# Experts of a mixture-of-experts trunk: gate and up in one product of 512 columns, halves of rows in 4 KB pieces, splits of 1024 columns, the last matrix wholly split

## The chip, the cores and the metric

The kernel runs on 1 core of one Trainium2 chip. The metric is the device time of one execution in microseconds (us). The time of the kernel before is the median of 3 runs; beside them stands one profiled execution, from which every row below comes.

## The reference

Two layers of a post-norm encoder: 512 tokens of 1024 channels. Each layer has a token mixer (an input projection, two attention branches, an output projection) and then the mixture of experts, which the change is about. For each token a router picks one group of four experts and the two best experts in it; every expert is a gated unit of 256 channels.

```python
def _moe(h, w_router, router_bias, w_gate, w_up, w_down):
    t = h.reshape(b * s, d)
    scores = jax.nn.sigmoid((t @ w_router).astype(jnp.float32))
    sel = scores + router_bias.astype(jnp.float32)
    ...
    combine = jnp.sum(jax.nn.one_hot(idx, N_EXPERTS, dtype=jnp.float32) * gate[..., None], 1)
    hg = jnp.einsum('td,edf->tef', t, w_gate)
    hu = jnp.einsum('td,edf->tef', t, w_up)
    act = jax.nn.silu(hg) * hu * combine[..., None].astype(t.dtype)
    y = jnp.einsum('tef,efd->td', act, w_down)
    return y.reshape(b, s, d)
```

Per layer there are 16 experts, each with w_gate and w_up of 1024 x 256 and w_down of 256 x 1024 numbers, all fp32: three matrices of 1 MB, 48 MB per layer.

## The kernel before

**Products in halves.** An fp32 product is made from three cheaper ones. A matrix W is split into H, its copy rounded to the type fp32r, and L = W - H, also kept as fp32r; the activations are split in the same way, and the product is the sum xH·wH + xH·wL + xL·wH (`gemm3`, L220 to L227). For a weight the rounding copy runs on ACT (`ACT.copy`, L215) and the subtraction on DVE (`V.tensor_sub`, L216), both in `wsplit`, in pieces of 512 columns (two blocks of 256). The pieces rotate through `NWH` = 6 buffers with the tag `wH` and 6 with `wL`.

**Experts.** The loop over the 16 experts stands at the end of `layer`. For expert e it runs `x_gate(e)`, `x_down(e - 1)`, `x_up(e)` and `x_split(e + 1)`.

- `x_load` gathers the up to 128 rows of the tokens of an expert from DRAM (`h2d`) into `xe`, with an indirect DMA that POOL issues (L1104).
- `x_split` turns `xe` with eight transposes on TensorE (`tp`) and splits the result from PSUM into `xH` on ACT (L343) and `xL` on DVE (L344), each in two halves of four blocks.
- `x_prod` (called by `x_gate` and `x_up`) loads and splits one matrix and multiplies: for each of 8 blocks of 128 channels three matmuls of 256 columns, 24 for gate and 24 for up. Gate's result goes through Silu on ACT (`ea`, L1129) and is multiplied by up's on DVE (L1136).
- `x_down` turns `ea`, makes `eT`, `eH` and `eL` of it, and multiplies with w_down in two stretches of 512 columns. The constant `DS` names the parts of w_down that are split; the first stretch is not split and is multiplied in plain fp32 (L1173, `mm<-raw,eT`), the second stretch takes six split matmuls. DVE scales the result (`ye`, L1174) and POOL stores it with an indirect DMA (L1178).

**What sets the order.** The code names the work; a scheduler orders each engine's instructions when the program is built, and every engine then runs its own list strictly in that order, with semaphores between engines. `tc.issue_after` is a hint to that scheduler. A branch (`overflow`, taken only when an expert has more than 128 tokens) stands ahead of expert `EIF` = 5 and closes the first of two scheduled stretches.

**Loads.** w_gate and w_up are read as eight blocks of 128 rows, so that each DMA piece is one row of 256 numbers (1 KB); rows of w_down are pieces of 4 KB. The raw matrices rotate through 4 buffers `raw` and 5 buffers `e8`. `AHEADW` lists twelve matrices that are loaded ahead of the loop.

**Ahead of the experts.** For each of four token tiles `tile_x1` normalizes the mixer's result and `tile_h2` normalizes it again with the layer's modulation (`norm`, columns up to `CUTH` = 896 on DVE, the other 128 on ACT and POOL) and writes it to `h2d`. `stats` reckons mean and deviation with DVE, and POOL makes the reciprocal root (L285, L286). The last tile's root feeds the router's scores `rt_sco`; from these DVE and TensorE reckon the list of rows `vt`, and with `vt` POOL gathers the first expert's tokens. TensorE waits for that.

## Time and profile before

| | |
|---|---|
| median of 3 runs | 1416.98 us (1414.26 to 1420.2) |
| the profiled execution's own time | 1411.59 us |
| its span in the trace | 1409.6 us |
| its mean granted TensorE clock | 0.954 of 2.4 GHz |

The profile shows one execution. A page gives the busy time of the engines; views by stage give the same for a stretch of the span, with the granted clock of TensorE and the load of the 16 DMA engines; a list in order of time shows single instructions, with the idle time ahead of them in square brackets and what ended it. TensorE is written PE, VectorE DVE, ScalarE ACT, GpSimd POOL. Matmuls overlap in the trace: from one's start to the next one's start is what one costs.

### The profile page before, as it was taken

How to read it: one execution, taken by the hardware profiler on the slowest of the kernel's cores; microseconds unless marked ns; L12 is line 12 of the kernel's file. 1: busy time of each engine (PE TensorE's matmuls, PEld its weight loads, DVE VectorE, ACT ScalarE, POOL GpSimd, SP SyncE). 2: the span in 40 equal slices, each digit the busy share in tenths (PEclk: the TensorE clock that was granted, in tenths of full speed). 3: DMA queues.
4: the chain of work that ended last, by engine and by line, in shares of the span. 5: the costliest groups of instructions: out<-in, count | busy, mean ns of one | idle time of the engine just before them, and what ended most of it. 6: DMA issues, size and time to landing. Idle time of an engine off the chain costs nothing. (4 is left out here: it accounts for less than half of the span.)

```text
span 1409.6 us, 21666 instructions
## 1 busy us (share of the span) xinstructions
PE 1283.9 (91%) x7953; PEld 1043.7 (74%) x7953; DVE 1018.3 (72%) x1944; ACT 717.1 (51%) x1504; POOL 292.8 (21%) x317
## 2 busy tenths in 40 slices
PE   4898999999998949899889899999999894989986
PEld 4787777677778848788659787767777794878862
DVE  5877877776367779899787876563336767879985
ACT  2344444555744337677554444455564532767760
POOL 1142000000013652222352200000000266122224
PEclk9799999999999969999999999999999996999998
DMA  9646555466066197899644454122215527779952
GB/s 319 213 151 248 197 179 172 150 190 192 30 195 209 60 299 255 275 346 333 240 144 150 150 179 150 61 75 76 75 51 173 196 75 255 263 255 347 355 207 79
DMA packets 182992, 266.77 MB, mean 189 GB/s; under 512 B 18665, under 2 KB 131721, under 8 KB 182880
## 3 DMA queue, kind: packets, MB, share of 16 engines
q1 hardware_dynamic: 159312, 225.46, 48.2%
q0 software_dynamic: 11456, 24.07, 4.9%
q10 hardware_dynamic: 12112, 15.78, 3.7%
q8 instruction: 66, 1.08, 0.3%
q14 instruction: 46, 0.38, 0.1%
HBM read 250.79 MB, written 27.30 MB: 197 GB/s over the span
## 5 line engine op out<-in xcount | busy, mean ns | idle before, releaser
L216 DVE TENSOR_TENSOR wL<-raw,wH 128x512 fp32r<-128x512 f32 x520 | 350.8, 703 | 75.6 <-ACT wH L215 64.3
L215 ACT CAST wH<-raw 128x512 fp32r<-128x512 f32 x520 | 318.3, 622 | 160.2 <-PE mm L1173 41.6
L225 PE MATMUL mm<-hH,wH 128*128 128x512 f32 x512 | 206.9, 404 | 0.0
L226 PE MATMUL mm<-hL,wH 128*128 128x512 f32 x512 | 202.9, 396 | 0.0
L227 PE MATMUL mm<-hH,wL 128*128 128x512 f32 x512 | 202.5, 395 | 0.0
L225 PE MATMUL mm<-wH,xH 128*128 128x256 f32 x512 | 150.5, 294 | 2.0 <-ACT xH L343 1.2
L227 PE MATMUL mm<-wH,xL 128*128 128x256 f32 x512 | 149.4, 292 | 0.7 <-DVE xL L344 0.7
L226 PE MATMUL mm<-wL,xH 128*128 128x256 f32 x512 | 147.4, 288 | 0.7 <-DVE wL L216 0.7
L249 DVE SCALAR_TENSOR_TENSOR acc<-araw,cond,acc 128x512 f32<-128x512 f32 x148 | 110.8, 749 | 5.4 <-DMA araw<-in_w_ada 2.2
L227 PEld LDWEIGHTS mm<-hH,wL 128*128 128x128 f32 x512 | 96.4, 188 | 21.0 <-issue 1.1
L225 PEld LDWEIGHTS mm<-hH,wH 128*128 128x128 f32 x512 | 96.7, 189 | 20.2 <-issue 1.2
L226 PEld LDWEIGHTS mm<-hL,wH 128*128 128x128 f32 x512 | 96.6, 189 | 19.2 <-issue 0.3
L225 PEld LDWEIGHTS mm<-wH,xH 128*128 128x128 f32 x512 | 100.5, 196 | 4.3 <-ACT xH L343 2.1
L226 PEld LDWEIGHTS mm<-wL,xH 128*128 128x128 f32 x512 | 100.0, 195 | 2.6 <-DVE wL L216 1.4
L227 PEld LDWEIGHTS mm<-wH,xL 128*128 128x128 f32 x512 | 99.7, 195 | 1.6 <-DVE xL L344 1.1
L225 PE MATMUL mm<-wH,hH 128*128 128x256 f32 (+1 forms) x272 | 81.5, 300 | 4.8 <-ACT hH L412 3.1
L227 PE MATMUL mm<-wH,hL 128*128 128x256 f32 (+1 forms) x272 | 80.8, 299 | 2.0 <-DVE hL L378 0.7
L226 PE MATMUL mm<-wL,hH 128*128 128x256 f32 (+1 forms) x272 | 80.3, 296 | 0.1
L1178 POOL DMA_INDIRECT y<-ye,vt x28 | 33.5, 1198 | 221.8 <-DVE ye L1174 221.8
L281 POOL DMA_DIRECT2D mod<-adar x8 | 4.2, 531 | 331.1 <-ACT adar L280 331.1
L1173 PE MATMUL mm<-raw,eT 128*128 128x512 f32 x128 | 65.9, 639 | 5.1 <-ACT eT L1156 3.1
L745 DVE TENSOR_TENSOR zB<-sB,biasB 128x256 f32<-128x256 f32 (+2 forms) x48 | 22.9, 488 | 59.9 <-PE sB L743 26.1
(319 smaller groups left out, 2873.9 us busy)
## 6 DMA issues: line engine op xcount, KB each, us to landing
araw<-in_w_ada SPq DMA_DIRECT2D x44, 1024.0 KB, 5.3
raw<-in_w_in SPq DMA_DIRECT2D x40, 1024.0 KB, 5.2
raw<-in_w_exp_gate SPq DMA_DIRECT2D x32, 1024.0 KB, 8.7
raw<-in_w_exp_up SPq DMA_DIRECT2D x28, 1024.0 KB, 9.7
raw<-in_w_exp_down SPq DMA_DIRECT2D x28, 1024.0 KB, 7.5
raw<-in_w_out SPq DMA_DIRECT2D x8, 1024.0 KB, 5.2
y<-y SPq DMA_DIRECT2D x16, 512.0 KB, 8.0
eraw<-in_w_ada SPq DMA_DIRECT2D x4, 1024.0 KB, 14.6
```

The costliest lines, as they stand in the source:

```text
L215: ACT.copy(H, raw(s))
L216: V.tensor_sub(L, raw(s), H.bitcast(F32))
L225: PE.matmul(o, lhsT=lH, rhs=rH, start=(i == 0), stop=False)
L226: PE.matmul(o, lhsT=lH, rhs=rL, start=False, stop=False)
L227: PE.matmul(o, lhsT=lL, rhs=rH, start=False, stop=(i == n - 1))
L249: last = V.scalar_tensor_tensor(acc, raw[:, k, :], ck, acc, op0=OP.mult, op1=OP.add)
L281: PO.dma_start(moddr[l, kind].rearrange("o (k n) -> (o k) n", n=P), r[0:8, :])
L745: V.tensor_add(z, s[:, :, 0:wid], biasB[g][:, ii::2, j0:j0 + wid])
L1173: PE.matmul(p, lhsT=a, rhs=w, start=(i == 0), stop=(i == len(todo) - 1))
L1178: st = PO.indirect_dma_start(out=y2, out_offset=bass.IndirectOffsetOnAxis(ap=vidx[:, e:e + 1], axis=0), in_=ye, in_offset=None, bounds_che ...
```

## The change

Gate and up of an expert become one product. `x_raw` loads half of the rows of both (512 of 1024) side by side into one buffer of 128 x 2 x 4 x 256: a partition holds four neighbouring rows, so that each DMA piece is 4 KB, and each half is two DMAs of 512 KB. `x_prod(e, h)` splits such a half in two pieces of 1024 columns, and multiplies with 512 columns at a time (256 of gate, 256 of up) into one PSUM tile `gu`; two calls make 24 matmuls. Since the rows of the contraction are now numbered 4p + k, the activations' columns are written in that order by `norm_mixed`, which takes the place of `norm` in `tile_h2` and writes with a step of 128 columns.

`x_wdown` splits all of w_down into one pair of buffers `dH`, `dL` (one of each for all experts, taken from the `e8` pool): the copy on ACT, the subtraction on POOL. `x_down` has 12 split matmuls and no plain ones. The loop is `x_prod(e, 0)`, `x_down(e - 1)`, `x_wdown(e)`, `x_prod(e, 1)`, `x_act(e)`, `x_split(e + 1)`. All other weights are split in pieces of 1024 columns too, in 3 buffers each. Ten pieces of 1 MB are loaded ahead in place of twelve.

```diff
@@ wsplit
-            h = 512 // shape[1] if shape[1] < 512 else 1
+            h = min(a, 1024 // shape[1])
@@ 
+        def norm_mixed(src, name, g, b, st, q):
+            m, r, nb = st
+            n = f4(name, [D])
+            o = n.rearrange("p (h k q) -> p h q k", h=2, k=4)
+            view = lambda z: z.rearrange("p (h q k) -> p h q k", h=2, k=4)
+            x, g, b = view(src), view(g), view(b)
+            v = slice(q, P)
+            ACT.activation(o[:, 1, v], x[:, 1, v], AF.Identity, bias=nb, scale=r)
+            for h, u in ((0, slice(0, P)), (1, slice(0, q))):
+                V.scalar_tensor_tensor(o[:, h, u], x[:, h, u], m, g[:, h, u], op0=OP.subtract, op1=OP.mult)
...
+            PO.tensor_tensor(o[:, 1, v], o[:, 1, v], g[:, 1, v], op=OP.mult)
...
-                n2 = norm(n, "h2", r_sc2, r_sh2, st, CUTH)
+                n2 = norm_mixed(n, "h2", r_sc2, r_sh2, st, QH)
@@ layer
+                src = [z[512 * w:512 * w + 512].rearrange("(p k) n -> p k n", k=4) for z in (gate, up)]
...
+                raw = wp.tile([P, 2, 4, 256], F32, tag="raw", name="raw", bufs=NRAW) if tag == "raw" else e8("raw8", [2, 4, 256])
+                for i in range(2):
+                    SY.dma_start(raw[:, i], src[i])
+                return lambda j: raw[:, :, 2 * j:2 * j + 2]
...
+            def x_prod(e, h):
...
+                for j in range(2):
+                    H = wp.tile([P, 2, 2, 256], F32R, tag="wH", name="wH", bufs=NWH)
+                    L = wp.tile([P, 2, 2, 256], F32R, tag="wL", name="wL", bufs=NWH)
+                    with ExitStack() as order:
+                        if e == 0:
+                            order.enter_context(tc.issue_after(order1.ins))
+                        ACT.copy(H, raw(j))
+                        V.tensor_sub(L, raw(j), H.bitcast(F32))
+                    for i in range(2):
+                        k = 4 * h + 2 * j + i
+                        for n, (x, w) in enumerate(((xH, H), (xH, L), (xL, H))):
+                            PE.matmul(p, lhsT=x[:, k, :], rhs=w[:, :, i], start=(k == 0 and n == 0), stop=(k == 7 and n == 2))
+            def x_act(e):
...
+                ACT.activation(a, p[:, 0], AF.Silu)
+                V.tensor_mul(a, a, p[:, 1])
...
+            def x_wdown(e):
+                raw = x_src(e, "down")
+                for k in range(2):
+                    w = raw(slice(k, k + 1))[:, 0]
+                    with ExitStack() as order:
+                        if e == 0:
+                            order.enter_context(tc.issue_after(order1.ins))
+                        ACT.copy(dH[:, k], w)
+                        PO.tensor_tensor(dL[:, k], w, dH[:, k].bitcast(F32), op=OP.subtract)
...
+                    for k in range(2):
+                        for n, (x, w) in enumerate(((eH, dH), (eH, dL), (eL, dH))):
+                            PE.matmul(p, lhsT=x[:, k], rhs=w[:, k, js], start=(k == 0 and n == 0), stop=(k == 1 and n == 2))
...
-                x_gate(e)
+                x_prod(e, 0)
                 if e > 0:
                     x_down(e - 1)
-                x_up(e)
+                x_wdown(e)
+                x_prod(e, 1)
+                x_act(e)
@@ constants
-HOLD = 10
+HOLD = 9
-DS = ((0, 1), (1, 1))
-WPAT = ("e8",) * 5 + ("raw",) * 4
+WPAT = ("e8",) * 3 + ("raw",) * 4
-CUTH = 896
+QH = 96
-NWH = 6
+NWH = 3
```

**Order on ACT and DVE, one expert in the middle of the second stretch of layer 0.** Before, ACT's list from one Silu to the last split of the next tokens (`wH` with the same `raw` number belong to one matrix; `xH_6895` is the split of the next expert's tokens):

```order
L1129 ACTIVATE ea_6814<-mm_6789 128x256
L1156 COPY eT_6819<-tp_6816 128x256
L343 CAST eH_6821<-tp_6816 128x256
L215 CAST wH_6855<-raw8_6841 128x512
L343 CAST xH_6895<-tp_6897 128x512
L215 CAST wH_6887<-raw8_6885 128x512
L215 CAST wH_6891<-raw8_6885 128x512
L215 CAST wH_6916<-raw8_6914 128x512
L215 CAST wH_6920<-raw8_6914 128x512
L215 CAST wH_6924<-raw8_6914 128x512
L215 CAST wH_6928<-raw8_6914 128x512
L343 CAST xH_6895<-tp_6904 128x512
```

Now, from the split of this expert's tokens (`xH_6144`) to that of the next one's (`xH_6246`). `gu_6163` is this expert's product, `wH_6223` and `wH_6233` its second half, `wH_6269` and `wH_6279` the next expert's first half, `eH_6190` belongs to the expert before it, `raw8_6214` is this expert's w_down:

```order
L360 CAST xH_6144<-tp_6146 128x512
L360 CAST xH_6144<-tp_6153 128x512
L1167 CAST wH_6223<-raw8_6220 128x1024
L1167 CAST wH_6233<-raw8_6220 128x1024
L1167 CAST wH_6269<-raw8_6266 128x1024
L360 CAST eH_6190<-tp_6187 128x256
L1167 CAST wH_6279<-raw8_6266 128x1024
L1189 CAST dH_4893<-raw8_6214 128x1024 x2
L1178 ACTIVATE ea_6243<-gu_6163 128x256
L360 CAST xH_6246<-tp_6248 128x512
```

The two copies `dH` stand ahead of the Silu `ea`, and the next tokens' split stands behind both; before, it stood right behind `eH`. On DVE before, in the same place:

```order
L1136 TENSOR_TENSOR ea_6814<-ea_6814,mm_6859 128x256
L216 TENSOR_TENSOR wL_6925<-raw8_6914,wH_6924 128x512
L344 TENSOR_TENSOR xL_6896<-tp_6904,xH_6895 128x512
L216 TENSOR_TENSOR wL_6929<-raw8_6914,wH_6928 128x512
L216 TENSOR_TENSOR wL_6987<-raw8_6984,wH_6986 128x512
L216 TENSOR_TENSOR wL_6991<-raw8_6984,wH_6990 128x512
L216 TENSOR_TENSOR wL_6995<-raw8_6984,wH_6994 128x512
L344 TENSOR_TENSOR eL_6965<-tp_6959,eH_6964 128x256
L216 TENSOR_TENSOR wL_6999<-raw8_6984,wH_6998 128x512
L1174 TENSOR_TENSOR ye_6968<-mm_6969,row_5072 128x512
L344 TENSOR_TENSOR xL_7039<-tp_7040,xH_7038 128x512
```

And now:

```order
L361 TENSOR_TENSOR xL_6145<-tp_6146,xH_6144 128x512
L361 TENSOR_TENSOR xL_6145<-tp_6153,xH_6144 128x512
L1168 TENSOR_TENSOR wL_6224<-raw8_6220,wH_6223 128x1024
L1168 TENSOR_TENSOR wL_6234<-raw8_6220,wH_6233 128x1024
L1168 TENSOR_TENSOR wL_6270<-raw8_6266,wH_6269 128x1024
L361 TENSOR_TENSOR eL_6191<-tp_6187,eH_6190 128x256
L1168 TENSOR_TENSOR wL_6280<-raw8_6266,wH_6279 128x1024
L1207 TENSOR_TENSOR ye_6194<-mm_6195,row_4885 128x512
L1207 TENSOR_TENSOR ye_6194<-mm_6203,row_4885 128x512
L1179 TENSOR_TENSOR ea_6243<-ea_6243,gu_6163 128x256
```

The split `eL` of the expert before stands behind three subtractions of 1024 columns.

**Order on POOL in the same place.** Before, stores and gathers take turns:

```order
L1178 DMA y2_125<-ye_6116,vt_5052 1024x1024
L1104 DMA xe_5074<-h2d0_4265,vt_5052 128x1024
L1178 DMA y2_125<-ye_6253,vt_5052 1024x1024
L1104 DMA xe_5075<-h2d0_4265,vt_5052 128x1024
L1178 DMA y2_125<-ye_6396,vt_5052 1024x1024
L1104 DMA xe_5076<-h2d0_4265,vt_5052 128x1024
```

Now two subtractions for each expert stand between them:

```order
L1190 TENSOR_TENSOR dL_4894<-raw8_6214,dH_4893 128x1024
L1211 DMA y2_125<-ye_6194,vt_4865 1024x1024
L1190 TENSOR_TENSOR dL_4894<-raw8_6214,dH_4893 128x1024
L1136 DMA xe_4889<-h2d0_4065,vt_4865 128x1024
L1190 TENSOR_TENSOR dL_4894<-raw_6316,dH_4893 128x1024
L1211 DMA y2_125<-ye_6296,vt_4865 1024x1024
```

**Order on POOL ahead of the experts of layer 0, from the last tile's first norm on.** Before:

```order
L325 TENSOR_TENSOR x1_4908<-x1_4908,row_4191 128x256
L326 TENSOR_TENSOR x1_4908<-x1_4908,row_4193 128x256
L285 TENSOR_SCALAR rstd_4927<-mv_4925 128x1
L286 TENSOR_TENSOR rstd_4927<-rstd_4927,c_mhalf_100 128x1
L308 TENSOR_SCALAR nb_4930<-mv_4925,rstd_4927 128x1
L325 TENSOR_TENSOR h2_4934<-h2_4934,row_4259 128x128
L326 TENSOR_TENSOR h2_4934<-h2_4934,row_4261 128x128
L1098 MEMSET xe_5074 128x1024
L1098 MEMSET xe_5075 128x1024
L1098 MEMSET xe_5076 128x1024
```

Now, from the same two instructions (`x1`) on:

```order
L342 TENSOR_TENSOR x1_4714<-x1_4714,row_4007 128x256
L343 TENSOR_TENSOR x1_4714<-x1_4714,row_4009 128x256
L1190 TENSOR_TENSOR dL_4894<-raw_4755,dH_4893 128x1024
L285 TENSOR_SCALAR rstd_4733<-mv_4731 128x1
L1190 TENSOR_TENSOR dL_4894<-raw_4755,dH_4893 128x1024
L286 TENSOR_TENSOR rstd_4733<-rstd_4733,c_mhalf_100 128x1
L308 TENSOR_SCALAR nb_4736<-mv_4731,rstd_4733 128x1
L326 TENSOR_TENSOR h2_4740<-h2_4740,row_4059 128x32x4
L327 TENSOR_TENSOR h2_4740<-h2_4740,row_4061 128x32x4
L1130 MEMSET xe_4887 128x1024
```

The two subtractions of expert 0 stand ahead of and behind the first step of the last tile's root (`rstd_4733`). It is the same in layer 1.

## Rows read from the trace of the kernel before

**Rows 1.** The page's first part: busy time of the engines over the span.

```profile
PE 1283.9 (91%) x7953; PEld 1043.7 (74%) x7953; DVE 1018.3 (72%) x1944; ACT 717.1 (51%) x1504; POOL 292.8 (21%) x317
```

**Rows 2.** By stage: stretch, length, busy per engine, PEclk, DMA share, GB/s.

```profile
500.00:517.00 17.00, 3.12 (x36) 2.73 (x36) 14.20 (x64) 1.68 (x4) 10.96 (x14) 0.50 0.86 268
...
600.00:620.00 20.00, 19.84 (x132) 16.93 (x131) 18.35 (x32) 15.39 (x29) 5.07 (x4) 1.00 1.02 345
...
640.00:660.00 20.00, 19.84 (x134) 16.92 (x133) 18.37 (x32) 15.41 (x30) 3.72 (x3) 1.00 1.02 358
```

**Rows 3.** In order of time (start, length): TensorE through one expert's period, layer 0.

```profile
600.29 1.98 PE L1173 MATMUL mm<-raw,eT 128*128 128x512 f32 x4
...
602.57 0.40 PE L1173 MATMUL mm<-wH,eL 128*128 128x512 f32 x1
...
602.81 0.40 PE L1173 MATMUL mm<-wH,eH 128*128 128x512 f32 x1
...
603.50 0.28 PE L225 MATMUL mm<-wH,xH 128*128 128x256 f32 x1
603.62 0.28 PE L226 MATMUL mm<-wL,xH 128*128 128x256 f32 x1
...
610.65 1.98 PE L1173 MATMUL mm<-raw,eT 128*128 128x512 f32 x4
```

**Rows 4.** In order of time: DVE and POOL at the end of layer 0's experts.

```profile
686.62 5.16 POOL L1295 TENSOR_TENSOR x<-x,y 128x1024 f32<-128x1024 f32 x2 [7.76 <-ACT y L1294]
687.07 2.50 DVE L216 TENSOR_TENSOR wL<-raw,wH 128x512 fp32r<-128x512 f32 x1 [1.27 <-ACT wH L215]
...
689.50 0.68 DVE L1174 TENSOR_TENSOR yk<-mm,row 128x512 f32<-128x512 f32 x1
```

**Rows 5.** Durations by line (ns min/median/max): ACT, DVE, POOL at 1024 columns, store.

```profile
L215 ACT CAST wHb<-raw x8: 1031/1046/1055, 417.5 to 1123.4; 128x1024 fp32r<-128x1024 f32 x8
...
L216 DVE TENSOR_TENSOR wLb<-raw,wHb x8: 1209/1217/1226, 437.2 to 1124.7; 128x1024 fp32r<-128x1024 f32 x8
...
L1295 POOL TENSOR_TENSOR x<-x,y x8: 2368/2508/2737, 686.6 to 1376.6; 128x1024 f32<-128x1024 f32 x8
...
L1178 POOL DMA_INDIRECT y<-ye,vt x28: 1168/1201/1207, 535.9 to 1355.4; - x28
```

**Rows 6.** Groups of instructions (busy us, mean ns): the small splits around an expert.

```profile
L216 DVE TENSOR_TENSOR wL<-raw,wH 128x512 fp32r<-128x512 f32 x520 | 350.8, 703 | 75.6 <-ACT wH L215 64.3 <-PE tp L336 4.6 <-PE pa L226 1.7
...
L344 DVE TENSOR_TENSOR xL<-tp,xH 128x512 fp32r<-128x512 f32 x64 | 43.8, 687 | 6.5 <-ACT xH L343 6.2
...
L343 ACT CAST xH<-tp 128x512 fp32r<-128x512 f32 x64 | 37.8, 594 | 31.7 <-PE tp L336 31.7
...
L344 DVE TENSOR_TENSOR eL<-tp,eH 128x256 fp32r<-128x256 f32 x32 | 13.6, 425 | 6.9 <-ACT eH L343 4.5
...
L343 ACT CAST eH<-tp 128x256 fp32r<-128x256 f32 x32 | 12.5, 390 | 0.0
...
L1129 ACT ACTIVATE ea<-mm 128x256 f32<-128x256 f32 x32 | 12.4, 386 | 2.8 <-PE mm L227 0.3
```

**Rows 7.** In order of time: POOL and DVE at the last tile ahead of layer 0's experts.

```profile
498.58 0.72 POOL L326 TENSOR_TENSOR x<-x,row 128x256 f32<-128x256 f32 x1
...
500.36 0.18 POOL L285 TENSOR_SCALAR rstd<-mv 128x1 f32<-128x1 f32 x1 [1.06 <-DVE mv L305]
...
500.63 1.30 POOL L286 TENSOR_TENSOR rstd<-rstd,c_mhalf 128x1 f32<-128x1 f32 x1
501.97 0.23 DVE L969 SCALAR_TENSOR_TENSOR rt_sco<-rt_sco,rstd,rrow 128x16 f32<-128x16 f32 x1 [0.44 <-POOL rstd L286]
...
510.98 1.44 POOL L1104 DMA_INDIRECT xe<-h2d,vt  x1 [4.19 <-DVE rt_cnt L1086]
```

**Rows 8.** DMA, stretch 1360 to 1380 us: GB/s in 40 slices, packets by size.

```profile
GB/s 229 213 147 254 377 426 393 393 385 401 434 369 303 246 320 385 410 410 401 385 434 401 361 188 74 16 98 385 360 172 328 360 287 115 8 0 0 0 0 0
DMA packets 1434, 5.24 MB, mean 262 GB/s; under 512 B 160, under 2 KB 160, under 8 KB 1432
```

More of the change, by code (lines that the diff above doesn't have):

```diff
@@ L1117, in x_split @@
                 XS[e] = xH, xL
-            def x_prod(e, w):
+            dH, dL = e8("dH", [2, D], F32R), e8("dL", [2, D], F32R)
+            GU = {}
+            def x_prod(e, h):
                 xH, xL = XS[e]
-                W = wsplit(x_src(e, w), x_shape(w), tag=tags.get((e, w)), behind=[order1] if (e, w) in BEHIND else [])
-                p = pmm([P, 256])
-                gemm3(p, range(8), lambda k: (xH[:, k, :], xL[:, k, :]), lambda k: W(k, slice(0, 256)))
-                return p
@@ L1126, in x_gate @@
-            def x_gate(e):
-                p = x_prod(e, "gate")
+                if h == 0:
+                    GU[e] = pat([P, 2, 256], "gu")
+                p = GU[e]
+                raw = x_src(e, h)
+                for j in range(2):
[6 more added lines that the diff above has]
+                        V.tensor_sub(L, raw(j), H.bitcast(F32))
+                    for i in range(2):
+                        k = 4 * h + 2 * j + i
+                        for n, (x, w) in enumerate(((xH, H), (xH, L), (xL, H))):
+                            PE.matmul(p, lhsT=x[:, k, :], rhs=w[:, :, i], start=(k == 0 and n == 0), stop=(k == 7 and n == 2))
@@ L1128, in x_gate @@
+            def x_act(e):
+                XS.pop(e)
+                p = GU.pop(e)
                 a = sc("ea", [256])
-                ACT.activation(a, p, AF.Silu)
+                ACT.activation(a, p[:, 0], AF.Silu)
+                V.tensor_mul(a, a, p[:, 1])
                 WD[e] = a
-            def x_up(e):
-                a = WD[e]
-                p = x_prod(e, "up")
-                XS.pop(e)
-                V.tensor_mul(a, a, p)
-                raw = x_src(e, "down")
-                if not callable(raw):
-                    raw = wraw(raw, x_shape("down"), tags[e, "down"])
-                W = {}
-                for j in range(2):
-                    for k in range(2):
-                        w = raw(slice(k, k + 1))[:, :, 512 * j:512 * j + 512]
-                        if (k, j) in DS:
-                            w = wsplit(lambda s: w, [1, 512], behind=[order1] if e < 2 else [])
-                            W[k, j] = w(0, slice(0, 512))
-                        else:
-                            W[k, j] = w[:, 0]
-                WD[e] = a, W
+            def x_wdown(e):
+                raw = x_src(e, "down")
+                for k in range(2):
[5 more added lines that the diff above has]
+                        PO.tensor_tensor(dL[:, k], w, dH[:, k].bitcast(F32), op=OP.subtract)
```

62 lines of the change are left out of this document (30 added, 32 removed).

## Prediction

> **What bounds the kernel now.** I read the page's totals first: TensorE is busy for 1283.9 of 1409.6 us, DVE for 72%, ACT for 51%, POOL for 21% [rows 1]. An average says little, so I went to the stages. In the middle of the experts TensorE is busy for 19.84 of 20 us at the full granted clock, DVE for 18.4, ACT for 15.4, POOL for 3.7 to 5.1, and the DMA engines are full as well, at 345 to 358 GB/s [rows 2]. In order of time one expert takes 610.65 - 600.29 = 10.36 us [rows 3], with TensorE never waiting. So there TensorE sets the pace, DVE and DMA stand close behind, and POOL is nearly free. Ahead of the experts it is the other way round: TensorE works 3.1 of 17 us [rows 2], waiting for a chain on POOL and DVE (the last tile's root, then the scores, then the gather) [rows 7]. Whatever lengthens that chain is added to the time as it stands.
>
> **TensorE's own work.** A matmul of 256 columns costs 0.12 us (603.50 to 603.62), one of 512 costs 0.23 (602.57 to 603.50 is four) [rows 3]. Gate and up were 48 x 0.12 = 5.76 us and become 24 x 0.23 = 5.52. The last matrix was 3.21 us (600.29 to 603.50) and becomes 12 x 0.23 = 2.76. That removes 0.69 us of an expert's 10.36, or 32 x 0.69 = 22 us in all, if TensorE goes on setting the pace. DVE loses ten subtractions of 512 columns (0.70 us) and gets four of 1024 (1.22): 2.1 us less. ACT loses ten copies and gets six of 1.05 (four `wH`, two `dH`), and no `eT`. POOL gets two subtractions of 1024 columns, whose nearest row is an addition of that size: 2.51 us, 2.37 to 2.74 [rows 5]. By sums every engine would fit into 9.7 us. But each list runs in order, and two things in the new lists are not free.
>
> **POOL and DVE get in each other's way.** At 686.62 POOL starts two additions of 1024 columns with both operands in SBUF. DVE starts a subtraction `wL` of 512 columns at 687.07 and needs 2.50 us for it, where 0.70 is usual: it ends when POOL's first addition has ended. At 689.50, while POOL's second one runs, DVE's `yk`, which reads one operand from PSUM, takes its ordinary 0.68 [rows 4, 6]. So a DVE subtraction with two operands in SBUF and a POOL one shut each other out for a whole instruction, and the change puts just these two kinds into every expert.
>
> **One expert's period, worked out.** I take the new lists of ACT, DVE and POOL shown with the change and lay the rows' durations along them. Time 0 is the first matmul of the expert, when the first half of `xH` is there.
> - TensorE's third matmul needs `xL` (0.69 on DVE [rows 6]) and starts at 0.8; the first half of gate and up ends at 0.8 + 10 x 0.23 = 3.1.
> - ACT makes the other half of `xH` until 0.59 and the first `wH` until 1.65. POOL's second `dL` of the expert before comes up at the same time: its first began when its `dH` was ready, 2.1 us before time 0, took 2.5, and a store took 1.2 [rows 5], which makes 1.7.
> - DVE now has three `wL` (3 x 1.22) and `eL` (0.43) to do, POOL one `dL` (2.51), and of these the four long ones exclude each other: 1.65 + 3.66 + 2.51 + 0.43 = 8.25, whoever goes first.
> - TensorE has the second half's first six matmuls, four of w_down's and two more until then, and waits; the other eight of w_down need `eL` and start at 8.3. The fifth of them is the last that reads the first half of `dH`; it starts at 9.22 and lasts 0.40: 9.62.
> - Only then ACT may overwrite `dH`, which is a single buffer: two copies until 11.75. Behind them in ACT's list stand the Silu (0.39) and the next tokens' `xH` (0.59) [rows 5, 6]: 12.73. The next expert starts at 12.8.
>
> That is 2.4 us more than 10.36. Without the lock the same walk gives `eL` at 5.97, w_down's eight at 6.14, `dH` until 9.6 and a period of 10.6: the wait for the single `dH` and the Silu behind it alone eat what TensorE saves. In the second stretch (experts 5 to 15) the lists repeat in this form; in the first (0 to 4) they differ, with the same subtractions in them. I count 14 of 16 experts, leaving out the first, whose weights are split while TensorE waits, and the last. 28 x 2.4 = 67 us. Bounds: with POOL at 2.37 and 12 experts, 24 x 2.2 = 53; with 2.74 and 16, 32 x 2.7 = 86; without the lock 28 x 0.25 = 7.
>
> **Ahead of the experts.** POOL's list there has expert 0's two `dL` ahead of and behind `rstd`. Before, `x` ended at 499.30, `rstd` ran at 500.36, the root from 500.63 and the scores' step at 501.97 [rows 7]. Now the first `dL` runs from 499.3 to 501.8, `rstd` until 502.0, the second `dL` until 504.5, and the root ends about 0.6 later or 1.3, as it did beside DVE's work: 505.1 to 505.8 in place of 501.9. I take 3.5 us later (bounds 2.5 and 5); scores, list and gather (510.98) follow it, and TensorE waits for them. In both layers 7 us. `norm_mixed` itself has four DVE instructions for two, over the same columns, mostly under TensorE's work of other tiles; its writes with a step of 128 columns have no row, so 0 to 1 us for the last tile, in the bounds above.
>
> **The rest.** After the last expert TensorE has nothing left to hide `dL`: two POOL subtractions and a part of the row additions behind them are bare. I take 2 us for each layer, 0 to 5. Splits of 1024 elsewhere save DVE 0.1 to 0.2 us each, where TensorE mostly sets the pace, and make each first matmul wait 0.4 us longer: -1 us a layer, -3 to +2. Fewer matrices loaded ahead cost nothing as long as an expert takes 10 us or more; the deeper of the remaining buffers hold seven matrices.
>
> Sum: 1411.6 (the profiled execution; span 1409.6 and 2 us around it) + 67 + 7 + 4 - 2 = 1487.6. The median of the runs shown is 5.4 us above that execution, so **1493 us**.
>
> **Rivals.**
> - *TensorE keeps the pace* (faster). If POOL's subtractions fall where DVE has PSUM work, and the Silu's chain is shorter than I reckon, 22 us go, the 7 us ahead of the experts come, -2 elsewhere: 1394.6, and 1400 as a median. For it: DVE's PSUM work is about 3.6 us an expert, long enough for one `dL`; I do place one of the two there. Against it: the other one, and `dH`'s single buffer, for which I see no cover.
> - *The lock is short, the loop remains.* Period 10.6: 1411.6 + 7 + 7 + 2 - 2 = 1426, median 1431. It decides if POOL lets DVE in within an instruction; the 2.50 us row speaks against it.
> - *Loads set the pace* (no change). An expert moves 10.36 us x 0.351 MB/us = 3.64 MB now [rows 2, 3]. If pieces of 4 KB moved no faster than the 358 GB/s of now, TensorE could gain only to 10.17 us: 32 x 0.19 = 6 us off, 9 on: about 1415 and 1420. Against it: a stretch with nearly all packets of 2 to 8 KB shows 401 to 434 GB/s where it is full [rows 8]. The Trainium skill (SBUF — State Buffer, section "A bandwidth-pool intuition that's wrong (but worth ruling out)") gives about 358 GB/s from HBM to one core; by that rule this rival's time would be the best that can be had. The trace does not agree with it, at 434 GB/s in a slice of 0.5 us.
> - *Worse.* TensorE's granted clock falls in the new waits, or the first stretch's lists wait longer: over 1530.
>
> **How the numbers follow.** Forecast 0.62, TensorE's pace 0.12, short lock 0.13, loads 0.05, worse 0.08. The range of 8 in 10 goes from the no-change rival to the forecast's upper bound (1411.6 + 86 + 10 + 10 + 4 + 5): 1415 to 1527; what it leaves out is the faster rival and what is worse. What differs by less than 0.5% could not be told from no change in a measurement of this kernel: faster 0.12, same 0.05, slower 0.83.
>
> **What would show it.** In the changed kernel's profile a step of the middle experts should be about 12.8 us long, TensorE busy for some 75% of it, `wL` of 1024 columns with a maximum near 3.7 us or a mean well above 1.22, and DVE's `eL` the last thing that TensorE waits for in w_down. ACT's `dH` should wait for TensorE, and the first matmul of each expert for ACT's `xH`. Ahead of the experts `rstd` and the root should stand 2 to 4 us apart. Should `wL` stay at 1.22 us, the lock is wrong; should the period be under 10 us, the loop through `dH` is.

## Result and profile after

The changed kernel takes 1519.35 us, the median of four runs of 1515.76 to 1524.73, against 1415.67 us before, four runs too (1414.26 to 1420.20): 1.0735 times as long, 95% interval 1.0705 to 1.0765. Its profiled execution has a span of 1514.5 us where 1409.6 stood before, so 104.9 us have to be found. The page's totals of the changed kernel answer to [rows 1]:

```profile
PE 1297.8 (86%) x7249; PEld 1016.1 (67%) x7249; DVE 1054.8 (70%) x1668; ACT 693.8 (46%) x1244; POOL 460.8 (30%) x383
```

TensorE's work has hardly grown (1284 to 1298 us), and no engine is full: what came is waiting. The groups of instructions (line, engine, operation, operands, count, then busy us and mean ns, then idle time ahead and what ended it) name the place:

```profile
L1168 DVE TENSOR_TENSOR wL<-raw,wH 128x1024 fp32r<-128x1024 f32 x128 | 224.2, 1776 | 26.4 <-ACT wH L1167 22.5 <-DMA raw<-in_w_exp_gate 0.4
...
L1190 POOL TENSOR_TENSOR dL<-raw,dH 128x1024 fp32r<-128x1024 f32 x64 | 154.1, 2410 | 165.4 <-ACT dH L1189 164.5
...
L1172 PE MATMUL gu<-wL,xH 128*128 128x512 f32 x256 | 107.9, 421 | 43.3 <-DVE wL L1168 43.3
...
L1189 ACT CAST dH<-raw 128x1024 fp32r<-128x1024 f32 x64 | 64.0, 1047 | 62.8 <-PE mm L1206 61.2
```

In this kernel `wL` of the experts has a mean of 1.776 us, where a subtraction of that size takes 1.22 [rows 5], and TensorE waits 43.3 us for it.

To see where the 104.9 us lie I put five marks into each layer of both traces: the first matmul of the attention's output, `vt` (end of the routing), and the Silu of experts 1, 6 and 15. All from the rows in order of time, us:

| stretch | layer 0 before, after | layer 1 before, after | sum of differences |
|---|---|---|---|
| start to the output's first matmul (layer 0) | 430.1, 433.5 | | +3.3 |
| output's first matmul to `vt` | 79.8, 93.2 | 80.6, 90.0 | +22.7 |
| `vt` to Silu 1 | 20.9, 25.9 | 20.6, 26.8 | +11.2 |
| Silu 1 to Silu 6 (five experts, the branch) | 58.4, 78.9 | 59.8, 79.9 | +40.6 |
| Silu 6 to Silu 15 (nine) | 93.2, 111.2 | 93.2, 111.4 | +36.2 |
| Silu 15 to layer 1's output, or the end | 423.5, 419.3 | 49.5, 44.6 | -9.1 |

The third and the last line belong together: before, the Silu came behind gate alone, and now behind gate and up, some 4.5 us later in an expert; together they hold 2.1 us. The 3.3 us of the first line are no part of the change that I can hold on to: among kernels below with the same code there, that matmul starts at 430.8 to 437.0.

**The middle experts.** TensorE in 20 us (columns as in [rows 2], whose line 640 to 660 is the one to compare) and one period in order of time (start, length, engine, line, operation, count, [idle before, and what ended it]):

```profile
640.00:660.00 20.00, 17.49 (x81) 12.98 (x80) 17.07 (x18) 13.03 (x18) 12.04 (x7) 1.00 0.88 326
```

```profile
644.68 0.53 PE L1172 MATMUL gu<-wH,xH 128*128 128x512 f32 x1 [0.41 <-ACT xH L360]
650.15 0.50 PE L1172 MATMUL gu<-wL,xH 128*128 128x512 f32 x1 [1.70 <-DVE wL L1168]
657.06 0.50 PE L1172 MATMUL gu<-wH,xH 128*128 128x512 f32 x1 [0.40 <-ACT xH L360]
```

```profile
646.09 6.27 DVE L1168 TENSOR_TENSOR wL<-raw,wH 128x1024 fp32r<-128x1024 f32 x3
652.29 0.41 DVE L361 TENSOR_TENSOR eL<-tp,eH 128x256 fp32r<-128x256 f32 x1
```

```profile
646.09 4.00 DVE L1168 TENSOR_TENSOR wL<-raw,wH 128x1024 fp32r<-128x1024 f32 x1
```

```profile
643.02 2.38 POOL L1190 TENSOR_TENSOR dL<-raw,dH 128x1024 fp32r<-128x1024 f32 x1 [4.42 <-ACT dH L1189]
...
646.59 2.41 POOL L1190 TENSOR_TENSOR dL<-raw,dH 128x1024 fp32r<-128x1024 f32 x1
```

```profile
654.26 2.00 ACT L1189 CAST dH<-raw 128x1024 fp32r<-128x1024 f32 x2 [1.58 <-PE mm L1206]
```

One expert takes 657.06 - 644.68 = 12.38 us. Three `wL` need 6.27 us in place of 3.7, because the first of them (4.00) sits through POOL's `dL` of 2.41. TensorE then waits 1.70 us, at the second of the twelve matmuls in the second half of gate and up, and at the start of each expert 0.40 for `xH`.

**Ahead of the experts.** POOL and DVE at the last tile, which answer to [rows 7]:

```profile
510.78 0.72 POOL L343 TENSOR_TENSOR x<-x,row 128x256 f32<-128x256 f32 x1
511.47 2.34 POOL L1190 TENSOR_TENSOR dL<-raw,dH 128x1024 fp32r<-128x1024 f32 x1
513.90 0.74 POOL L285 TENSOR_SCALAR rstd<-mv 128x1 f32<-128x1 f32 x1
514.72 2.77 POOL L1190 TENSOR_TENSOR dL<-raw,dH 128x1024 fp32r<-128x1024 f32 x1
517.45 0.54 POOL L286 TENSOR_TENSOR rstd<-rstd,c_mhalf 128x1 f32<-128x1 f32 x1
```

```profile
518.03 0.23 DVE L986 SCALAR_TENSOR_TENSOR rt_sco<-rt_sco,rstd,rrow 128x16 f32<-128x16 f32 x1 [2.62 <-POOL rstd L286]
```

From the end of `x` to the scores' step it was 501.97 - 499.30 = 2.67 us; now it is 518.03 - 511.50 = 6.53. But that is 3.9 of the 13.4 us of this stretch. The tiles ahead of it have grown too: from the first to the last tile's first score step it is 46.0 and 42.3 us (layers 0 and 1) where it was 39.5, and the first of these steps stands 30.1 and 29.7 us behind the output's first matmul, where it stood 27.2.

**The first stretch.** Here an expert takes up to 19.0 us (Silu 2 to 3). DVE, POOL and TensorE in the worst place, and the stages around it:

```profile
569.80 5.95 DVE L1168 TENSOR_TENSOR wL<-raw,wH 128x1024 fp32r<-128x1024 f32 x1 [0.26 <-ACT wH L1167]
```

```profile
569.98 4.68 POOL L1190 TENSOR_TENSOR dL<-raw,dH 128x1024 fp32r<-128x1024 f32 x2
```

```profile
575.80 0.50 PE L1172 MATMUL gu<-wL,xH 128*128 128x512 f32 x1 [2.66 <-DVE wL L1168]
...
589.53 0.63 PE L1172 MATMUL gu<-wL,xH 128*128 128x512 f32 x1
589.95 0.63 PE L1172 MATMUL gu<-wH,xL 128*128 128x512 f32 x1
...
596.03 0.39 PE L1172 MATMUL gu<-wH,xH 128*128 128x512 f32 x1
596.26 0.39 PE L1172 MATMUL gu<-wL,xH 128*128 128x512 f32 x1
```

```profile
572.00:576.00 4.00, 0.93 (x3) 0.49 (x4) 4.00 (x2) 0.00 (x0) 2.66 (x2) 1.00 0.04 16
576.00:580.00 4.00, 3.49 (x9) 2.44 (x9) 1.78 (x3) 0.14 (x1) 0.00 (x0) 0.63 0.53 172
...
588.00:592.00 4.00, 3.92 (x9) 3.15 (x10) 2.93 (x5) 1.38 (x2) 0.92 (x1) 0.50 0.93 348
```

Two `dL` run one behind the other, one `wL` waits through both (5.95 us), TensorE works 0.93 of 4 us, and in the stretch behind it the granted clock is 0.63, further on 0.50, its lower level of 1.2 GHz. A matmul of 512 columns then costs 0.42 us (589.53 to 589.95) in place of 0.23 (596.03 to 596.26). 34 of the 180 such matmuls between Silu 1 and Silu 6 of layer 0 have a recorded length of 0.6 us or more, as at 589.53; by these steps that is some 34 x 0.19 = 6.5 us, an estimate. So the lock is paid twice here, as a wait and as a slower TensorE behind it.

### The profile page after: what moved, and what is told of

Read it like the earlier page. It is cut to its first block, busy times and chain, and to the rows that moved or that the text cites. A ratio compares the mean times of both kernels' runs of the same rounds, so it can differ in the third digit from the quotient of the medians.

```text
span 1514.5 us, 19632 instructions
## 1 busy us (share of the span) xinstructions
PE 1297.8 (86%) x7249; PEld 1016.1 (67%) x7249; DVE 1054.8 (70%) x1668; ACT 693.8 (46%) x1244; POOL 460.8 (30%) x383
## 5 line engine op out<-in xcount | busy, mean ns | idle before, releaser
L1168 DVE TENSOR_TENSOR wL<-raw,wH 128x1024 fp32r<-128x1024 f32 x128 | 224.2, 1776 | 26.4 <-ACT wH L1167 22.5
L1190 POOL TENSOR_TENSOR dL<-raw,dH 128x1024 fp32r<-128x1024 f32 x64 | 154.1, 2410 | 165.4 <-ACT dH L1189 164.5
L1167 ACT CAST wH<-raw 128x1024 fp32r<-128x1024 f32 x128 | 134.5, 1054 | 100.0 <-PE gu L1172 76.9
L216 DVE TENSOR_TENSOR wL<-raw,wH 128x1024 fp32r<-128x1024 f32 x100 | 123.6, 1237 | 81.0 <-ACT wH L215 68.1
L215 ACT CAST wH<-raw 128x1024 fp32r<-128x1024 f32 x100 | 104.6, 1048 | 88.6 <-PE mm L226 44.6
L1172 PE MATMUL gu<-wL,xH 128*128 128x512 f32 x256 | 107.9, 421 | 43.3 <-DVE wL L1168 43.3
L1172 PE MATMUL gu<-wH,xH 128*128 128x512 f32 x256 | 110.4, 431 | 10.9 <-ACT xH L360 10.9
L225 PEld LDWEIGHTS mm<-hH,wH 128*128 128x128 f32 x512 | 97.4, 190 | 19.4 <-issue 0.3
L1172 PE MATMUL gu<-wH,xL 128*128 128x512 f32 x256 | 108.1, 422 | 0.2
L1189 ACT CAST dH<-raw 128x1024 fp32r<-128x1024 f32 x64 | 64.0, 1047 | 62.8 <-PE mm L1206 61.2
L1172 PEld LDWEIGHTS gu<-wL,xH 128*128 128x128 f32 x256 | 51.2, 200 | 60.4 <-DVE wL L1168 51.2
L1172 PEld LDWEIGHTS gu<-wH,xH 128*128 128x128 f32 x256 | 50.7, 198 | 24.8 <-ACT xH L360 16.6
```

Source lines behind the costliest of these rows:

```text
L215: ACT.copy(H, raw(s))
L216: V.tensor_sub(L, raw(s), H.bitcast(F32))
L225: PE.matmul(o, lhsT=lH, rhs=rH, start=(i == 0), stop=False)
L1167: ACT.copy(H, raw(j))
L1168: V.tensor_sub(L, raw(j), H.bitcast(F32))
L1172: PE.matmul(p, lhsT=x[:, k, :], rhs=w[:, :, i], start=(k == 0 and n == 0), stop=(k == 7 and n == 2))
```

## Experiments

Times are medians; a period is the mean over eight experts from Silu 6 to Silu 14, the same in both layers within 0.06 us. Before it is 10.35, after 12.35.

**1. POOL takes no part** (`e1_dve_sub`).

```
-                        PO.tensor_tensor(dL[:, k], w, dH[:, k].bitcast(F32), op=OP.subtract)
+                        V.tensor_sub(dL[:, k], w, dH[:, k].bitcast(F32))
```

> The changed kernel with one edit: the subtraction that makes dL runs on VectorE and no longer on GpSimd. Theory (GpSimd's dL and VectorE's wL shut each other out, and what that costs sets the period of an expert): the wL return to 1.22 us each, but VectorE gets two more instructions of 1.22 us, so its own sum per expert is 4 x 1.22 + 2 x 1.22 + 2 x 0.69 + 0.42 + 2 x 0.69 + 0.42 = 10.9 us. Expected: a period of 11.0 to 11.5 us in place of 12.35, some 28 x 1.1 = 31 us less over both layers, and about 3 us less in each layer ahead of the experts, where dL of expert 0 no longer stands on GpSimd among the routing steps: 1475 to 1492 us. Rival (the one pair dH, dL sets the period: ScalarE may not write it before TensorE has read the last expert's): the period stays at 12.35 or grows by the added VectorE work, 1515 to 1555 us.

1466.37 us, ratio to before 1.036 (1.032 to 1.040); period 10.70. The mean of `wL` is 1.219 us again. DVE in one expert of this kernel:

```profile
650.57 2.35 DVE L1168 TENSOR_TENSOR wL<-raw,wH 128x1024 fp32r<-128x1024 f32 x2
...
656.78 2.35 DVE L1190 TENSOR_TENSOR dL<-raw,dH 128x1024 fp32r<-128x1024 f32 x2
```

53 us come back, more than expected: 29 in the nine experts of the two layers' second stretch, 19 in the first, where fewer waits also leave fewer matmuls at the lower clock (22 of 180, counted in the same way). From the last tile's first score step to `vt` it is 14.2 us, 2.8 and 3.8 less. The period lies under the sum of 10.9 that I had made: DVE is busy for 10.09 of the 10.70 us, since instructions in a row overlap in the records (two subtractions take 2.35, not 2.44), and TensorE waits 0.8 us per expert, for `xH` and `xL`.

**2. POOL stays, with one operand of SBUF** (`e2_one_operand`). The low half of the last matrix is left out here.

```
-                        PO.tensor_tensor(dL[:, k], w, dH[:, k].bitcast(F32), op=OP.subtract)
+                        PO.tensor_scalar(dL[:, k], w, 0.0, None, op0=OP.mult)
```

> The changed kernel with GpSimd's subtraction replaced by a multiplication of w with zero: it reads one operand of SBUF where it read two. The low half of the last matrix is left out of the result this way; all transfers, buffers, products and waits stay. Theory of the exclusion (it needs two SBUF operands on GpSimd's side): the wL return to 1.22 to 1.35 us although GpSimd works beside them, VectorE's three wL take 3.7 to 4.2 us in place of 6.27, and the period falls from 12.35 to 10.6 to 11.2 us: 28 x 1.45 = 41 us less, 1470 to 1485 us. Rival (the one pair dH, dL sets the period, or GpSimd slows VectorE whatever it reads): the period stays within 0.3 us of 12.35 and the time within 1510 to 1522 us.

1465.07 us, ratio 1.033 (1.030 to 1.036); period 10.36, under the range that I had given. One period of this kernel (stage, then rows of DVE and POOL in order of time):

```profile
683.82:694.17 10.35, 9.98 (x47) 7.63 (x47) 8.33 (x11) 7.62 (x11) 7.69 (x4) 1.00 0.97 368
```

```profile
685.24 1.23 DVE L1168 TENSOR_TENSOR wL<-raw,wH 128x1024 fp32r<-128x1024 f32 x1
```

```profile
683.33 2.77 POOL L1190 TENSOR_SCALAR dL<-raw 128x1024 fp32r<-128x1024 f32 x1
```

The other `dL` of an expert, and the `wL` recorded just ahead of it, from an earlier period:

```profile
669.13 1.23 DVE L1168 TENSOR_TENSOR wL<-raw,wH 128x1024 fp32r<-128x1024 f32 x1
...
669.16 3.84 POOL L1190 TENSOR_SCALAR dL<-raw 128x1024 fp32r<-128x1024 f32 x1 [0.87 <-issue]
```

And the matmul that starts the next expert:

```profile
694.17 0.50 PE L1172 MATMUL gu<-wH,xH 128*128 128x512 f32 x1 [0.37 <-ACT xH L360]
```

POOL is busier than before the edit (7.69 of 10.35 us), the one pair `dH`, `dL` is still there, and ACT still waits 1.57 us for it; yet the period has fallen by 2.0 us. So DVE's waits for POOL set the period of 12.35, and the single pair does not. The lock itself is not gone: the `dL` at 669.16 takes 3.84 us where the other takes 2.77, so here POOL waits, and the period doesn't grow by it, and a `wL` that starts 0.02 us behind POOL (552.66, in the first stretch) still takes 2.11. The edit changes the operation along with the operands, so this run doesn't say which of the two it is. From Silu 1 to Silu 6 it is 64.6 and 65.3 us: of the first stretch's 40.6 us, 28.9 are the exclusion's, with the clock that falls behind its waits, and 11.7 are not taken away by this edit. Where it is still longest against before is the third expert (Silu 2 to 3, 15.2 and 15.5 us where it was 10.35) and the one at the branch (Silu 4 to 5, 19.9 and 20.3 where it was 15.2 and 16.7); Silu 1 to 2 is 3.7 shorter. What this kernel loses again is the last expert, 17.1 and 15.0 us. The kernels without POOL's part below have 14.4 to 15.3 there (experiment 5), so POOL need not be the reason, and it is not shown.

**3. Two pairs of `dH` and `dL`** (`e3_two_pairs`).

```
-            dH, dL = e8("dH", [2, D], F32R), e8("dL", [2, D], F32R)
+            DW = [[e8(f"{n}{i}", [2, D], F32R) for n in ("dH", "dL")] for i in range(2)]
...
+                dH, dL = DW[e % 2]
...
-WPAT = ("e8",) * 3 + ("raw",) * 4
+WPAT = ("e8",) + ("raw",) * 4
...
```

> The changed kernel with two pairs of dH and dL, used in turn; the two tiles for them are taken from the weight tiles (three of the eight-kilobyte tiles that hold loaded weights become one, and two pieces fewer are loaded ahead of expert 0). Theory of a loop through the one pair (ScalarE's dH waits for TensorE's last products of the expert before): that wait, 1.60 us per steady expert, goes, dL starts earlier, and the period falls to where VectorE is set by its own sum of 8.4 us and what the exclusion adds, about 11.0 to 11.6 us: 28 x 1.0 = 28 us less, 1480 to 1500 us. Rival (the exclusion alone sets the period): it stays within 0.2 us of 12.35, 1512 to 1524 us. Second rival (five weight tiles in place of seven are too few): TensorE and ScalarE wait for DMA, the period is above 12.5, 1525 to 1570 us.

1500.59 us, ratio 1.059 (1.056 to 1.062). The period is 12.37: the rival's, to 0.02 us. The profiled execution is 16.5 us shorter than the changed kernel's, and the largest parts are the first stretch (74.1 and 75.0 us for five experts, 9.7 less) and what follows the last Silu of a layer (12.5 less, with 4.6 more from `vt` to Silu 1). `dL` of expert 0 stands elsewhere now, but from the output's first matmul to `vt` it is 92.9 and 92.8 us where it was 93.2 and 90.0, so nothing is gained there. ACT and DVE of this kernel:

```profile
710.65 2.00 ACT L1190 CAST dH<-raw 128x1024 fp32r<-128x1024 f32 x2 [1.58 <-PE mm L1208]
```

```profile
702.50 3.99 DVE L1168 TENSOR_TENSOR wL<-raw,wH 128x1024 fp32r<-128x1024 f32 x1
```

ACT's wait is still there: its list now writes a pair one expert earlier, at the same place, behind the same matmuls. So this run doesn't show what the wait alone costs; with the run before it shows that more buffers don't help while `wL` takes 3.99.

**4. The norm as before** (`e5_norm_as_before`), with the columns reordered at TensorE's transposes.

```
-                n2 = norm_mixed(n, "h2", r_sc2, r_sh2, st, QH)
+                n2 = norm(n, "h2", r_sc2, r_sh2, st, CUTH)
...
-                    transposes(lambda i: xe[:, (4 * q + i) * P:(4 * q + i + 1) * P], p, 4)
+                    transposes(lambda i: xe.rearrange("p (h q k) -> p h k q", h=2, k=4)[:, q, i], p, 4)
...
```

> The changed kernel with the norm of the kernel before (contiguous writes, 896 columns on VectorE and 128 on ScalarE and GpSimd); the order of the columns that the 4 KB pieces need is made where TensorE transposes the gathered rows, by reading every fourth column. Theory (the mixed norm's strided halves cost VectorE 2.1 us in place of 1.16 in the second pass and some 0.4 in the first, once per tile of tokens, on the path to the routing): the distance of the tiles' score steps falls from 13.9 to 14.9 us to 12.5 to 13.1, 4 x 1.4 = 5.6 us less in each layer; the experts' period stays at 12.35: 1505 to 1511 us. Rival (the stage waits for something else, and strided reading costs TensorE more than it gives): 1514 to 1530 us, with transposes of xe longer than 0.60 us for four.

1508.75 us, ratio 1.064 (1.061 to 1.066); period unchanged. The second pass of the norm on DVE and POOL's part in the changed kernel, and DVE's second pass here:

```profile
1212.42 2.13 DVE L325 SCALAR_TENSOR_TENSOR h<-h,rstd,row 128x512 f32<-128x512 f32 x2
```

```profile
1212.60 1.28 POOL L326 TENSOR_TENSOR h<-h,row 128x128 f32<-128x128 f32 x1 [0.73 <-ACT h L321]
```

```profile
1193.11 1.15 DVE L340 SCALAR_TENSOR_TENSOR h<-h,rstd,row 128x896 f32<-128x896 f32 x1
```

With 1.15 in place of 2.13 us the first and the last tile are 39.7 us apart in both layers again, 6.3 and 2.6 less. This distance differs between kernels and layers with the same norm (42.3 to 48.3 us over the six kernels with `norm_mixed`, 38.1 to 43.2 over the seven with the norm as before), so a single pair of layers gives the size only roughly. The transposes of `xe` have a mean of 0.291 us in place of 0.282, which the experts' unchanged period doesn't show.

**5. The last matrix as before** (`e4_half_split`): `dH`, `dL` and POOL's part are gone.

```
...
+                H = wp.tile([P, 2, 512], F32R, tag="wH", name="wH", bufs=NWH)
+                L = wp.tile([P, 2, 512], F32R, tag="wL", name="wL", bufs=NWH)
...
+                        ACT.copy(H[:, k], w)
+                        V.tensor_sub(L[:, k], w, H[:, k].bitcast(F32))
...
+                        todo = ((eH[:, k], H[:, k]), (eH[:, k], L[:, k]), (eL[:, k], H[:, k])) if j else ((eT[:, k], raw[k][:, js]),)
...
```

> The changed kernel with the last matrix as in the kernel before: columns 512 to 1023 split by ScalarE and VectorE, columns 0 to 511 as one full-precision product; dH, dL and GpSimd's part are gone, all else stays. Theory (what the change costs comes mostly from the wholly split last matrix, through the exclusion of GpSimd and VectorE): VectorE's sum per expert is 4 x 1.22 + 2 x 0.68 + 2 x 0.69 + 0.42 + 2 x 0.69 + 0.42 = 9.8 us, TensorE's 5.5 + 3.2 + 1.4 = 10.1, so the period is 10.2 to 10.7 us in place of 12.36: 28 x 1.9 = 53 us less, about 4 us less in each layer ahead of the experts, and some 4 us less in each first stretch, where TensorE no longer falls to its lower clock as often: 1440 to 1465 us. Rival (the layout of gate and up, the halves or the splits of 1024 columns cost most): 1490 to 1520 us.

1465.82 us, ratio 1.038 (1.035 to 1.041): half of the loss goes with this matrix, as much as with POOL's part of it alone (experiments 1 and 2). The period is 11.04, above the range that I had given. With both put back (`e6_half_norm`):

> The changed kernel with the last matrix as in the kernel before and the norm as before, columns reordered at the transposes: what is left of the change is the product of 512 columns for gate and up, halves in 4 KB pieces, and splits of 1024 columns. By the two costs taken off: 10.6 us under the kernel that has only the last matrix put back, 1430 to 1455 us, so still 1 to 2.5 per cent slower than before, through a first stretch and a start of the experts that are longer. Rival (nothing of the cost is left, and the 0.24 us that TensorE saves per expert shows): 1405 to 1417 us.

1452.11 us, ratio 1.027 (1.025 to 1.030); period 11.05. Two periods of it:

```profile
642.00:664.00 22.00, 21.12 (x90) 14.99 (x89) 18.59 (x25) 14.16 (x22) 4.06 (x4) 1.00 0.94 334
```

TensorE is busy for 21.1 of 22 us, and yet an expert takes 0.7 us more than before. The stage's busy time hides a part of it, so I added up TensorE's steps over six experts (Silu 7 to 13), from one start to the next, without idle time. The 24 matmuls of gate and up take 6.42 us per expert, where the 48 of before took 5.90; with them comes idle time of 0.44 us, in which TensorE waits for `wL`:

```profile
654.24 0.50 PE L1172 MATMUL gu<-wL,xH 128*128 128x512 f32 x1 [0.68 <-DVE wL L1168]
```

Behind such a wait, and behind transposes, the first matmul of 512 columns takes 0.33 to 0.34 us and not 0.23. The last matrix is a little shorter (2.96 against 3.20). So 24 matmuls of 512 columns save nothing here over 48 of 256. The profiled execution of this kernel is 49.1 us longer than that of before (its median is some 39 us above); 20 of them lie in the nine experts of the two second stretches and 15 in the five of the first. What makes the waits, the next runs were to tell.

**6. What holds 11.05?** Transposes of the next expert ahead of the second half (`e8_half_early`), and splits of 512 columns in six buffers (`e10_small_splits`), each on the kernel with both put back:

```
...
                 x_wdown(e)
+                if e + 1 < NE:
+                    x_split(e + 1)
                 x_prod(e, 1)
```

> As the kernel with the last matrix and the norm put back, and with the transposes and splits of the next expert's rows placed ahead of the second half of gate and up in place of behind it. Theory (TensorE waits about 0.4 us at the start of each expert for ScalarE's xH, since the eight transposes end its list): that wait goes, 30 x 0.4 = 12 us less than with the transposes behind: 1418 to 1443 us. Rival (TensorE isn't the bound, or the earlier transposes wait for the gathered rows or for a bank): the same time within 4 us, or longer by up to 15.

1469.09 us, ratio 1.039; period 11.63: 17 us worse, where the rival had up to 15.

```
-            h = min(a, 1024 // shape[1])
+            h = 512 // shape[1] if shape[1] < 512 else 1
...
-                    H = wp.tile([P, 2, 2, 256], F32R, tag="wH", name="wH", bufs=NWH)
+                        H = wp.tile([P, 2, 256], F32R, tag="wH", name="wH", bufs=NWH)
...
-NWH = 3
+NWH = 6
```

> As the kernel with the last matrix and the norm put back (1452 us, a period of 11.0), with splits of 512 columns in six buffers in place of 1024 columns in three. Theory (the period of 11.0 in place of 10.35 comes from the buffers: ScalarE's next wH waits for TensorE to leave one of three, up to 2.1 us, and VectorE's wL is late by 0.7): the period falls to 10.2 to 10.6 us, 28 x 0.6 = 17 us less, 1428 to 1441 us. Rival (the product of 512 columns in halves sets the period, and twice as many splits add 8 x 0.68 - 4 x 1.22 = 0.6 us to VectorE): the period stays at 10.9 to 11.4, 1448 to 1464 us.

1450.56 us, ratio 1.025; the period alternates between 10.2 and 12.1, 11.13 in the mean. TensorE waits 0.77 us per expert in this kernel, for `xL` and `xH` and no longer for `wL`, and gate and up take 6.10 us without that. So neither the transposes' place nor pieces of 1024 columns in three buffers is the cause: the wait moves and stays. What would remove it stays open. One thing did come back: the first tile's score step stands 27.2 and 27.3 us behind the output's first matmul, as before the change, in place of 30.4 and 30.1 without this edit. The first lines of the cut change the split of all other weights as well, and at the attention's output splits of 1024 columns cost some 3 us.

**7. Weight tiles** (`e11_tiles`: five rotating tiles and twelve pieces ahead; `e12_tiles_small`: that and splits of 512).

```
-WPAT = ("e8",) * 3 + ("raw",) * 4
+WPAT = ("e8",) * 5 + ("raw",) * 4
```

> As the kernel with the last matrix and the norm put back, with the two tiles of dH and dL given back to the weights: five eight-kilobyte tiles rotate and twelve pieces are loaded ahead, as in the kernel before. Theory (the expert behind the branch on the overflow is late, 20.2 and 19.1 us in place of 15.2 and 16.6, because SyncE issues its loads only behind the branch for want of free tiles): that expert takes 15.5 to 17.5 us, expert 2 gains up to 2 us, the steady period stays at 11.0: 8 to 12 us less, 1440 to 1446 us. Rival (the delay is not in the loads): within 4 us of 1452.

1452.00 us, ratio 1.027; the expert at the branch takes 18.3 and 19.4 us (20.2 and 19.1 without the edit): no effect that shows, the theory falls.

> Both edits together: five tiles for the weights and splits of 512 columns in six buffers. What is then left of the change is the product of 512 columns, halves in 4 KB pieces, and the reordered columns at the transposes. If both theories hold the gains add up, 1418 to 1432 us, within 1.5 per cent of before; if neither does, 1448 to 1460 us.

1446.95 us, ratio 1.022 (1.019 to 1.025), the lowest median of all these kernels, 1 us under the range given for the case that neither helps, and still longer than before.

**8. Two repairs at once** (`e7_dve_norm`: DVE's subtraction and the norm as before).

> The changed kernel with two edits together: dL subtracted on VectorE (period 10.7 us, 1466 us alone) and the norm as before with the columns reordered at the transposes (1509 us alone, 10.6 us less). Theory (the two costs lie one behind the other, the norm ahead of the experts, the exclusion within them): they add up, 1452 to 1460 us. Rival (VectorE, now fuller, or another wait takes one of the gains back): 1462 to 1470 us.

1457.62 us, ratio 1.033. The sum of the two single gains gives 1455.8: they add up, so the two costs lie one behind the other.

**9. Shorter pieces on POOL** (`e13_short_pieces`).

```
-                        PO.tensor_tensor(dL[:, k], w, dH[:, k].bitcast(F32), op=OP.subtract)
+                        for c in (slice(0, 512), slice(512, 1024)):
+                            PO.tensor_tensor(dL[:, k, c], w[:, c], dH[:, k, c].bitcast(F32), op=OP.subtract)
```

> The changed kernel with GpSimd's dL in four instructions of 512 columns per expert in place of two of 1024. Theory (the two engines shut each other out for whole instructions, and what VectorE loses is the sum of GpSimd's time that falls into its three wL, about one dL of 2.4 us): the pieces take 1.2 to 1.4 us each, VectorE may slip in between two of them, but loses the same sum, so the three wL take 5.9 to 6.6 us and the period stays at 12.0 to 12.6: 1505 to 1530 us. Rival (what is lost hangs on the length of one piece that VectorE waits for): the three wL take 4.6 to 5.2 us and the period falls to 11.0 to 11.5, 28 x 1.1 = 31 us less, 1480 to 1495 us.

1544.51 us, ratio 1.094; periods of 12.6 and 14.1, 13.56 in the mean. DVE and POOL of this kernel:

```profile
719.00 4.24 DVE L1168 TENSOR_TENSOR wL<-raw,wH 128x1024 fp32r<-128x1024 f32 x1
```

```profile
718.37 3.78 POOL L1191 TENSOR_TENSOR dL<-raw,dH 128x512 fp32r<-128x512 f32 x3
```

The three `wL` take 6.51 us, as the theory had it, but the time is above both forecasts: in the middle experts DVE doesn't get in between two pieces. It waits through all three that are ready, 3.78 us, where it waited through one `dL` of 2.41.

## Why the prediction was right, and what it had wrong

The sign, the main mechanism and the range held; 1493 was 26 us short of 1519. Its sum had 67 + 7 + 4 - 2 = 76 us, and the trace has 76.8 + 22.7 + 2.1 + 3.3 = 104.9. That the time lies within the range is partly luck: the 22.7 us ahead of the experts are above the 10 and 4 us that bounded `dL` with the norm and the splits, and it is the wide bound of 86 for the experts that covers them.

- *The exclusion* is shown. Taking POOL itself away (experiment 1), or its subtraction with two SBUF operands (experiment 2), brings the mean of `wL` back to 1.22 to 1.26 us and takes 53 to 54 us off the time. That each engine waits for the other's whole instruction is more than the runs show: with one operand on POOL it holds in part.
- *The period*: 12.35, forecast 12.8. Its growth was 2.0 us per expert and not 2.4. The walk took POOL's 2.51 from additions [rows 5], and `dL` takes 2.41; and it has TensorE wait for `eL` in the last matrix, where it waits for `wL` in the second half of gate and up. So TensorE is busy for 87% of that stage and not for some 75%.
- *The loop through the single `dH`*: the period "without the lock 10.6" came out as 10.36 in experiment 2. The prediction's own terms give that, and its 10.6 doesn't follow from them: `eL` is ready at 1.65 + 3.66 + 0.43 = 5.74 and TensorE comes to its eight matmuls at 3.1 + 12 x 0.23 = 5.86, not at 6.14, and carried on that gives 10.3. That TensorE's saving is lost again holds: 10.36 is no better than 10.35. But the larger part was never saved. Gate and up take 5.98 us without idle time there, where 5.52 was forecast and 5.90 stood before, and the last matrix 2.84, where 2.76 was forecast. What the last matrix does give, 0.36, goes into the wait of 0.36 for `xH`. That this wait comes from the single pair was argued and is not shown, since ACT's wait stayed with two pairs (experiment 3).
- *28 experts alike* was the mis-sized term among the experts. The nine of the second stretch cost 36.2 us in both layers, where 2.4 each makes 43.2; the five of the first cost 40.6, where 2.4 each makes 24. Experiment 2 splits the 40.6: 28.9 by the exclusion, 2.9 us per expert, where two `dL` can fall on one `wL` and the clock goes down behind the wait; 11.7 by something else, which none of the runs names (weight tiles, tried in experiment 7, changed nothing at the branch). The prediction had the falling clock only as a rival of 0.08.
- *Ahead of the experts* is where most is missing: 22.7 us, forecast 7. `dL` around `rstd` is right (3.9 and 4.1 us, from the last tile's first score step to `vt`, forecast 3.5; experiment 1 takes 2.8 and 3.8 of it away). `norm_mixed` was counted as 0 to 1 us for the last tile alone; it has 2.13 us in place of 1.15 on DVE in every tile, and DVE stands in each tile's path: 6.5 and 2.8 us (experiment 4 takes off 6.3 and 2.6, and 10.6 us of the time). Splits of 1024 were counted as a gain of 1 us a layer, within -3 to +2; at the attention's output they cost 2.9 and 2.5 (`e10_small_splits`).
- *The last expert*, 4 us in both layers, can't be read by itself: with the shift of the Silu it comes to 2.1.
- *Loads* and *TensorE keeps the pace* didn't come: the DMA share is 0.88 in the stage where it was 1.02, with 326 GB/s in place of 358 [rows 2]. "Fewer matrices loaded ahead cost nothing" was not tried on the changed kernel itself; on the one with both put back (experiment 7) giving tiles and pieces back changed no time.

## What to carry over

Before a subtraction goes to an idle POOL, look at what DVE does in that stretch: if both read two operands from SBUF, DVE can pay POOL's length, here twice as long per element (2.41 us against 1.22), and idle time on POOL is no room. A gain of a few per cent on the bounding engine came to nothing here, since new waits for the engines behind it and longer steps took it back, and a layout that one stage wants is paid in the stage that writes it (here once per tile, on the path). More than a third of the loss (the 1.027 of the kernel with the last matrix and the norm put back, out of 1.0735) is located but not explained.
